# Head of a hybrid decoder block: a third weight chunk is loaded before x, first loads are cut in two, half of the token parts are made in quarters

## The chip, the core and the metric

The kernel runs on one core of a Trainium2 chip. The core has a matrix engine (TensorE, PE in the profile, with its weight loads as PEld), a vector engine (VectorE, DVE), an activation engine (ScalarE, ACT), a general engine (GpSimd, POOL) and a queue that issues most of the transfers (SyncE, SP). The metric is the time of one execution on the device, in microseconds; lower is better.

## What is computed

One layer: a pre-norm with two parallel mixers (a convolution module and a sparse attention with three branches), cross-attention into 256 memory tokens, a gated feed-forward, and a last norm. There are 256 tokens of 1024 features, all in float32. Cut to what matters here, where only the start of the work is touched:

```python
h = rms_norm(x, norm_mix_g[l])
x = x + hybrid_mixer(h, w_in[l], ...)         # u = h @ w_in[:, :2048] comes first in the kernel
h = rms_norm(x, norm_x_g[l])
x = x + cross_attention(h, mem, xq_w[l], xkv_w[l], xo_w[l])

def cross_attention(h, mem, wq, wkv, wo):
    k, v = jnp.split(mem @ wkv, 2, axis=-1)   # k = mem @ wkv[:, :1024] is made first of all
    ...
```

The keys `k` of the cross-attention need only `mem` and weights, so the kernel makes them first, while `x` is being loaded and normed.

## The kernel before

**Products.** Every weight matrix is cut into chunks of 256 output columns (k0 to k3 for the keys, u0 to u7 for the convolution's input, and so on). A chunk is 1024x256 floats, 1 MiB; it is loaded in two halves of 512 KiB (lines 211-212, 219). For most chunks both operands are split into a high part (ScalarE copies with rounding, line 184, or line 303 for data) and a low part (the difference, on VectorE or GpSimd, line 186, or line 304 for data), and `rows` (line 248) issues three sweeps for each half: high by high, high by low, low by high, eight matmuls each of 128x128 weights by 256 columns (line 259). One chunk is six such sweeps, 48 matmuls. k0 alone is multiplied in plain float32 (`whole`, line 280, matmuls at line 289), straight from the loaded `mem_t` and `k0w`, so that it needs no parts.

**Start of the program.** Lines 362-364 issue eight float32 warm-up products on ones. Lines 373-374 load the memory tokens `mem_t` in four pieces of 256 KiB from ScalarE's queue. Line 375 loads k0 in four pieces of 256 KiB from SP's queue (`ahead`, line 207-210), line 376 loads k1 in two halves. Then follow on SP's queue x in two halves (line 378), two small constant tables cp of 128x186 and pp of 128x528 floats (lines 379-380), and k2, k3 and u0 (lines 381-382). The first `Sqrt` table is asked for at line 383 on ScalarE.

**Order of the work.** `kx(0)` multiplies k0 by the memory tokens. Lines 391-393 make the memory tokens' parts in two halves of four 128-row blocks each. `kx(1)` follows. Then x is squared on ScalarE (line 397), summed over its eight blocks on VectorE to two (line 399), summed over features on TensorE (the `rn` product, line 347), rooted on ScalarE (line 349) and inverted on VectorE (line 350). Eight VectorE operations scale x into `hf` (line 405), and line 407 makes the parts of the normed tokens in four pieces x0 to x3. k2, k3 and the u chunks follow.

A planner orders the instructions of each engine by the times of its own model; each engine then runs its list in that order and waits by semaphores. `first[name]` names operations behind which the split of a weight half has to stand in the list of its engine (line 183): before, the second half of k2 stands behind the root and the inverse of the norm (line 401), the second half of k3 behind x0's part and a scaling (line 409), and the first half of u0 behind the parts x2 (line 410).

Of the kernel before, what the change touches and what calls it, by code (L numbers as in the profile page):

```python
# [97 lines left out]
def tile_hybrid_block(  # L98
# [16 lines left out]
    nc = tc.nc  # L115
# [6 lines left out]
    def long(name, slot, shape=(P, NB, S), dt=F32):  # L122

        return sb.tile(list(shape), dt, tag=f"L{slot}", name=name)

    def longs(names, slots, dt=F32R):
        return [long(n, i, dt=dt) for n, i in zip(names, slots)]
# [64 lines left out]
    first, splits, paused = {}, {}, []  # L192
# [11 lines left out]
    def ahead(name, slot):  # L204

        w = held[name] = long(f"{name}w", slot, (P, NB, 256))
        if name == "k0":
            for i in range(4):
                nc.sync.dma_start(w[:, 2 * i:2 * i + 2], w0[i])
            return  # L210
        for i in range(2):
            nc.sync.dma_start(w[:, 4 * i:4 * i + 4], wst[CHUNK_AT[name]][:, 4 * i:4 * i + 4])
# [12 lines left out]
    def half(src, name):  # L225
        w = small(name, list(src.shape), tag="w", bufs=4)
        nc.sync.dma_start(w, src)
        return split(w, list(src.shape), name)
# [73 lines left out]
    def part(hi, lo, src):  # L302
        copy = nc.scalar.activation(hi, src, AF.Copy)
        low = nc.vector.tensor_tensor(out=lo, in0=src, in1=f(hi), op=ALU.subtract)
        return copy, low
# [37 lines left out]
    def rooted_all(sqs, name, tag):  # L343

        ps = aux(f"rn_{name}", [P, S], "o", 1)
        for i, sq in enumerate(sqs):
            nc.tensor.matmul(ps, lhsT=ones, rhs=sq, start=i == 0, stop=i == len(sqs) - 1)
        r = small(f"r_{name}", [P, S], tag=tag[0], bufs=tag[1])
        root = nc.scalar.activation(r, ps, AF.Sqrt, bias=eps1)
        first[name] = root, nc.vector.reciprocal(r, r)  # L350
        return r
# [18 lines left out]
    kxh, kxl = longs(("kxh", "kxl"), (4, 5))  # L370
    mem, h = (memh, meml), (hh, hl)
    mem_t, hf = longs(("mem_t", "hf"), (6, 9), F32)
    for i in range(4):
        nc.scalar.dma_start(mem_t[:, 2 * i:2 * i + 2], memt[i])
    ahead("k0", 10)
    ahead("k1", 14)
    for i in range(2):
        nc.sync.dma_start(xt_t[:, 4 * i:4 * i + 4], xt[:, 4 * i:4 * i + 4])
    nc.sync.dma_start(cpt, cp)
    nc.sync.dma_start(ppt, pp)  # L380
    for name, slot in (("k2", 12), ("k3", 11), ("u0", 13)):
        ahead(name, slot)
    roots("roots0")

    def kx(j):
        ps = gemm(f"k{j}", mem) if j else whole("k0", mem_t)
        with behind(*first["x3"] if j > 1 else ()):
            part(kxh[:, 2 * j:2 * j + 2], kxl[:, 2 * j:2 * j + 2], ps[:])

    kx(0)  # L390
    for i in range(2):
        hs = slice(4 * i, 4 * i + 4)
        part(memh[:, hs], meml[:, hs], mem_t[:, hs])
    kx(1)
    for i in range(2):
        hs = slice(4 * i, 4 * i + 4)
# [1 line left out]
    for n in (4, 2):  # L398
        nc.vector.tensor_tensor(out=sq[:, 0:n], in0=sq[:, 0:n], in1=sq[:, n:2 * n], op=ALU.add)
    r1 = rooted_all([sq[:, 0], sq[:, 1]], "1", ("sg", 3))  # L400
    first["k2_1"] = first["1"]
    for i in range(4):
        hs = slice(2 * i, 2 * i + 2)
        for kb in (2 * i, 2 * i + 1):
# [2 lines left out]
        first[f"x{i}"] = part(hh[:, hs], hl[:, hs], hf[:, hs])  # L407
        if i == 2:
            first["k3_1"] = first["x0"][0], vec
    for name, i in (("u0_0", 2), ("u0_1", 3), ("u1_0", 3), ("u1_1", 3)):  # L410
        first[name] = first[f"x{i}"]
    for j in range(2, 4):
        kx(j)
# [885 lines left out]
    for i in range(early):  # L1299
# [4 lines left out]
        else:  # L1304
            for c in range(2):
                w = half(wfo[i, :, 2 * c:2 * c + 2], f"fo{i}_{c}")
# [9 lines left out]
    for i in range(early, NF // 2):  # L1316
        w = half(wfo[i, :, 0:2], f"fo{i}_0")
# [180 lines left out]
```

## Time and profile before

| | us |
|---|---|
| median of 3 runs | 531.47 (531.02 to 531.73) |
| the profiled execution, its own time | 532.03 |
| its span, from the first to the last instruction | 530.0 |
| TensorE busy in the span | 522.3 |
| VectorE busy | 433.9 |
| ScalarE busy | 343.7 |
| GpSimd busy | 156.0 |

The profile gives for every engine its busy time in the span. Matmuls overlap and their ends are modelled, so small holes between starts don't show as idle time of TensorE; starts of successive groups show them. A row of the timeline has the start in us, the length in us, the engine, the line, the operation, the tiles (out<-in), the shapes, a count, and in brackets the idle time of the engine just before with what ended it. A line such as L184 or L259 belongs to a helper that serves many chunks, so the tile's name tells which.

### The profile page before, as it was taken

Reading aid. Unit: us, or ns where it says so; the run is one execution under the profiler, and the core shown is the slowest. Engines: PE = TensorE matmul, PEld = TensorE weight load, DVE = VectorE, ACT = ScalarE, POOL = GpSimd, SP = SyncE. Lnnn points to the kernel's source line nnn. Section 1 sums busy time; section 2 is a strip of 40 time slices with the busy share of each in tenths; the row PEclk is TensorE's granted clock in tenths of the full one; section 3 lists DMA queues with packets and bytes.
Section 4 is the critical chain, followed back from the end, with each engine's and each line's share of the span. In section 5 each row is a group of like instructions: output and inputs, shape, how many; then the busy total and the mean of one; then the engine's idle time right before and its main releaser. Section 6 shows DMA issues by size and latency. Waiting matters only on the chain.

```text
span 530.0 us, 11121 instructions
## 1 busy us (share of the span) xinstructions
PE 522.3 (99%) x4316; PEld 504.8 (95%) x4316; DVE 433.9 (82%) x871; ACT 343.7 (65%) x599; POOL 156.0 (29%) x110
## 2 busy tenths in 40 slices
PE   9999999999999999999999999999999999999995
PEld 8999999999999999999999999999999999988884
DVE  4868999899978898975869676697889888878985
ACT  4685466787656888789446664665556665657553
POOL 0069999999961200200004000330000000000001
PEclk9999999999999999999999999999999999999998
DMA  8927954664355544347765643847765567455622
GB/s 309 416 98 267 350 185 161 202 216 160 121 182 177 178 141 135 105 147 213 233 205 171 235 153 119 236 167 258 218 199 198 198 233 226 157 137 173 220 88 80
DMA packets 30740, 101.55 MB, mean 192 GB/s; under 512 B 3296, under 2 KB 5856, under 8 KB 30304
## 3 DMA queue, kind: packets, MB, share of 16 engines
q1 hardware_dynamic: 29104, 96.99, 54.0%
q0 software_dynamic: 864, 2.62, 3.1%
q10 hardware_dynamic: 720, 1.23, 0.6%
q8 instruction: 34, 0.56, 0.5%
q14 instruction: 18, 0.15, 0.1%
HBM read 99.59 MB, written 1.25 MB: 190 GB/s over the span
## 4 chain that ended last, share of the span: by engine, by line
PE 60%; DVE 1%; ACT 0%; issue 0%; ACTq 0%; DVEq 0%
PE ps_f L259 23%; PE fo L1254 6%; PE ps_xo L259 4%; PE ps_v L259 4%; PE ps_pw L259 4%; PE ps_wo L259 4%; PE ps_xq L259 4%; PE m L1254 4%; PE xs L989 1%; PE xo_ps L989 1%; PE o L819 1%; PE pt_a L798 1%; PE s L753 1%; PE o L816 1%; PE pt_b L798 0%; PE o L810 0%
## 5 line engine op out<-in xcount | busy, mean ns | idle before, releaser
L437 DVE SCALAR_TENSOR_TENSOR yp<-vt,ppt,yp 128x256 f32<-128x256 f32 x204 | 81.6, 480 | 0.2
L259 PE MATMUL ps_f<-g,f_1h 128*128 128x256 f32 x352 | 44.4, 277 | 0.0
L259 PE MATMUL ps_f<-g,f_0h 128*128 128x256 f32 x352 | 43.8, 277 | 0.0
L259 PEld LDWEIGHTS ps_f<-g,f_1h 128*128 128x128 f32 x352 | 42.1, 188 | 0.1
L259 PEld LDWEIGHTS ps_f<-g,f_0h 128*128 128x128 f32 x352 | 41.8, 188 | 0.0
L184 ACT ACTIVATE f_0h<-f 128x1024 fp32r<-128x1024 f32 x22 | 23.3, 1057 | 16.8 <-issue 5.7
L186 DVE TENSOR_TENSOR f_1l<-f,f_1h 128x1024 fp32r<-128x1024 f32 x22 | 27.4, 1248 | 6.8 <-ACT f_1h L184 5.9
L184 ACT ACTIVATE f_1h<-f 128x1024 fp32r<-128x1024 f32 x22 | 23.3, 1060 | 14.3 <-PE ps_f L259 10.6
L186 DVE TENSOR_TENSOR f_0l<-f,f_0h 128x1024 fp32r<-128x1024 f32 x22 | 26.7, 1212 | 1.7 <-ACT f_0h L184 1.7
L186 POOL TENSOR_TENSOR u_0l<-u,u_0h 128x1024 fp32r<-128x1024 f32 x7 | 17.4, 2479 | 30.4 <-DVE kt L523 30.4
L259 PE MATMUL ps_f<-g,f_0l 128*128 128x256 f32 x176 | 23.9, 277 | 0.0
L259 PE MATMUL ps_f<-g,f_1l 128*128 128x256 f32 x176 | 23.7, 277 | 0.0
L259 PEld LDWEIGHTS ps_f<-g,f_0l 128*128 128x128 f32 x176 | 21.9, 188 | 0.0
L1220 DVE TENSOR_TENSOR ab<-ps_f,r 128x512 f32<-128x512 f32 x22 | 15.1, 689 | 8.3 <-PE ps_f L259 8.3
L259 PEld LDWEIGHTS ps_f<-g,f_1l 128*128 128x128 f32 x176 | 21.7, 188 | 0.0
L773 ACT ACTIVATE p<-p,mins 128x256 f32<-128x256 f32 x32 | 15.9, 502 | 8.4 <-DVE mins L758 8.4
L1138 POOL DMA_DIRECT2D spare<-in_wfo_dram x1 | 0.9, 866 | 65.1 <-DVE ab L1220 65.1
L186 POOL TENSOR_TENSOR u_1l<-u,u_1h 128x1024 fp32r<-128x1024 f32 x7 | 17.9, 2560 | 0.0
L449 POOL TENSOR_TENSOR yt<-yt,vw 128x512 f32<-128x512 f32 x13 | 17.1, 1312 | 0.0
L1222 ACT ACTIVATE sl<-ab 128x256 f32<-128x256 f32 x22 | 9.1, 417 | 11.1 <-DVE ab L1220 11.1
L1296 POOL TENSOR_TENSOR x<-y,gf 128x512 f32<-128x512 f32 x2 | 2.6, 1298 | 46.1 <-issue 46.1
L259 PE MATMUL ps_u<-hh,u_0h 128*128 128x256 f32 x128 | 16.1, 276 | 0.0
(614 smaller groups left out, 1632.1 us busy)
## 6 DMA issues: line engine op xcount, KB each, us to landing
f<-in_wst_dram SPq DMA_DIRECT2D x44, 512.0 KB, 4.3
fo<-in_wfo_dram SPq DMA_DIRECT2D x16, 512.0 KB, 3.5
u<-in_wst_dram SPq DMA_DIRECT2D x14, 512.0 KB, 7.9
q<-in_wst_dram SPq DMA_DIRECT2D x8, 512.0 KB, 4.1
ga<-in_wst_dram SPq DMA_DIRECT2D x8, 512.0 KB, 3.5
gc<-in_wst_dram SPq DMA_DIRECT2D x8, 512.0 KB, 3.7
v<-in_wst_dram SPq DMA_DIRECT2D x8, 512.0 KB, 5.8
pw<-in_wst_dram SPq DMA_DIRECT2D x8, 512.0 KB, 4.8
```

What stands on the lines that cost most here:

```text
L184: copy = nc.scalar.activation(hi, w, AF.Copy)
L186: splits[name] = copy, eng.tensor_tensor(out=lo, in0=w, in1=f(hi[:]), op=ALU.subtract)
L259: mm = nc.tensor.matmul(ps[:, b], lhsT=lhsT, rhs=rhs, start=row + b + kb == 0, stop=kb == NB - 1 and row == 2 and b == 1)
L437: nc.vector.scalar_tensor_tensor(out=out[:, i] if t == ts[-1] else acc[i], in0=v, scalar=w, in1=acc[i], op0=ALU.mult, op1=ALU.add)
L449: nc.gpsimd.tensor_tensor(out=yt[:, 0:2], in0=yt[:, 0:2], in1=pr, op=ALU.add)
L753: nc.tensor.matmul(s1, lhsT=qh(hd, 1), rhs=t[:, g].rearrange("p b t -> p (b t)"), start=i == 0, stop=i == 1)
L773: exp.append(nc.scalar.activation(p1[k][:, br], p1[k][:, br], AF.Exp, scale=-1.0, bias=mins[:, hd, 1, br:br + 1], accum_out=sums[:, hd, 1, ...
L798: mm = nc.tensor.transpose(ps[:, i], src, ident)
L989: mm = nc.tensor.matmul(o, lhsT=lhsT, rhs=rhs, start=n == 0, stop=n == len(order) - 1)
L1220: scaled[:] = [nc.vector.tensor_tensor(out=ab, in0=ps, in1=rf.unsqueeze(1).to_broadcast([P, 2, S]), op=ALU.mult)]
L1222: silu = nc.scalar.activation(sl, ab[:, 0], AF.Silu)
L1254: mm = nc.tensor.matmul(o, lhsT=a[x], rhs=b[w], start=start and n == 0, stop=stop and n == 2)
```

## The change

It does five things, all in the first microseconds of the program: the first of k0's four pieces and the first of the memory tokens' four pieces are loaded as two single blocks each; k2 is loaded ahead of x on SP's queue; the second half of the memory tokens' parts is made in two quarters; the split of k2's second half no longer has to stand behind the norm's root and inverse; and the split of u0's first half stands behind the parts x1 instead of x2.

```diff
         if name == "k0":
-            for i in range(4):
+            for k in range(2):
+                nc.sync.dma_start(w[:, k], w0[0, :, k])
+            for i in range(1, 4):
                 nc.sync.dma_start(w[:, 2 * i:2 * i + 2], w0[i])
             return
...
-    for i in range(4):
+    for k in range(2):
+        nc.scalar.dma_start(mem_t[:, k], memt[0, :, k])
+    for i in range(1, 4):
         nc.scalar.dma_start(mem_t[:, 2 * i:2 * i + 2], memt[i])
     ahead("k0", 10)
     ahead("k1", 14)
+    ahead("k2", 12)
     for i in range(2):
         nc.sync.dma_start(xt_t[:, 4 * i:4 * i + 4], xt[:, 4 * i:4 * i + 4])
     nc.sync.dma_start(cpt, cp)
     nc.sync.dma_start(ppt, pp)
-    for name, slot in (("k2", 12), ("k3", 11), ("u0", 13)):
+    for name, slot in (("k3", 11), ("u0", 13)):
         ahead(name, slot)
...
     kx(0)
-    for i in range(2):
-        hs = slice(4 * i, 4 * i + 4)
+    for hs in (slice(0, 4), slice(4, 6), slice(6, 8)):
         part(memh[:, hs], meml[:, hs], mem_t[:, hs])
     kx(1)
...
     r1 = rooted_all([sq[:, 0], sq[:, 1]], "1", ("sg", 3))
-    first["k2_1"] = first["1"]
...
-    for name, i in (("u0_0", 2), ("u0_1", 3), ("u1_0", 3), ("u1_1", 3)):
+    for name, i in (("u0_0", 1), ("u0_1", 3), ("u1_0", 3), ("u1_1", 3)):
         first[name] = first[f"x{i}"]
```

## The prediction

> **What bounds the kernel now.** I read the page first: the span's engines, and the chain of work that ended last.
>
> ```profile
> span 530.0 us, 11121 instructions
> ...
> PE 522.3 (99%) x4316; PEld 504.8 (95%) x4316; DVE 433.9 (82%) x871; ACT 343.7 (65%) x599; POOL 156.0 (29%) x110
> ...
> PE 60%; DVE 1%; ACT 0%; issue 0%; ACTq 0%; DVEq 0%
> ```
>
> TensorE is busy for 522.3 of 530.0 us, and no other engine has a share of the chain worth the name. So the change can win only what TensorE loses before the u chunks, and it can lose whatever it makes TensorE wait. Next came the view by stretches, to see whether a hole lies in the part that the change touches. Its columns are the stretch, its length, busy time and count of each engine, the granted clock, the DMA share and its rate.
>
> ```profile
> core 0: us, PE busy (x) PEld busy (x) DVE busy (x) ACT busy (x) POOL busy (x), PEclk, DMA share, GB/s
> 5.00:10.00 5.00, 5.00 (x24) 4.21 (x24) 1.34 (x2) 2.13 (x3) 0.00 (x0) 1.00 1.02 392
> ...
> 15.00:20.00 5.00, 4.53 (x35) 4.25 (x35) 4.17 (x5) 3.27 (x5) 0.00 (x0) 1.00 1.02 415
> ```
>
> The second of these stretches has the hole (4.53 of 5.00); the clock is whole and the transfers run all the time (share 1.02). TensorE's timeline shows where it is:
>
> ```profile
> 4.37 7.20 PE L289 MATMUL ps_k<-mem_t,k0w 128*128 128x256 f32 x32
> ...
> 15.18 1.10 PE L259 MATMUL ps_k<-meml,k_1h 128*128 128x256 f32 x8
> 16.12 1.10 PE L259 MATMUL ps_k<-memh,k_1l 128*128 128x256 f32 x8
> 17.70 1.10 PE L347 MATMUL rn<-xtsq,ones 128*128 128x256 f32 x4 [0.47 <-DVE xtsq L399]
> 18.45 1.28 PE L259 MATMUL ps_k<-memh,k_0h 128*128 128x256 f32 x8
> 19.57 1.07 PE L259 MATMUL ps_k<-meml,k_0h 128*128 128x256 f32 x8
> 20.48 1.07 PE L259 MATMUL ps_k<-memh,k_0l 128*128 128x256 f32 x8
> ```
>
> A sweep of eight takes 0.94 us from start to start in k1 (15.18 to 16.12). The next could have started at 16.12 + 0.94 = 17.06, and the norm's product starts at 17.70. So 0.64 us is lost (0.47 is what the modelled ends leave of it), because x's sum of squares is late and k2's weights, which could have filled the time, come after x. That is the largest sum at stake: 0.64 of 532.03 us of the profiled execution's own time, 0.12%. The same rows show two paces: 0.94 us for eight in k1, 0.91 in k2.
>
> ScalarE's timeline tells when the transfers land, since several of its operations wait for nothing else:
>
> ```profile
> 2.63 1.28 ACT L171 ACT_TABLE_LOAD   x1 [2.63 <-issue]
> ...
> 5.58 1.06 ACT L303 ACTIVATE memh<-mem_t 128x1024 fp32r<-128x1024 f32 x1 [1.45 <-DMA mem_t<-in_memt_dram]
> 8.80 1.06 ACT L303 ACTIVATE memh<-mem_t 128x1024 fp32r<-128x1024 f32 x1 [2.16 <-DMA mem_t<-in_memt_dram]
> 9.98 1.06 ACT L184 ACTIVATE k_0h<-k1w 128x1024 fp32r<-128x1024 f32 x1
> ...
> 13.21 1.06 ACT L397 ACTIVATE xtsq<-xtsq 128x1024 f32<-128x1024 f32 x1 [0.43 <-DMA xtsq<-in_xt_dram]
> 14.51 1.06 ACT L397 ACTIVATE xtsq<-xtsq 128x1024 f32<-128x1024 f32 x1 [0.23 <-DMA xtsq<-in_xt_dram]
> 16.65 1.06 ACT L184 ACTIVATE k_0h<-k2w 128x1024 fp32r<-128x1024 f32 x1 [1.08 <-DMA k2w<-in_wst_dram]
> ...
> 20.17 1.04 ACT L184 ACTIVATE k_0h<-k3w 128x1024 fp32r<-128x1024 f32 x1
> ...
> 25.75 1.14 ACT L303 ACTIVATE hh<-hf 128x512 fp32r<-128x512 f32 x2
> 26.79 1.05 ACT L184 ACTIVATE u_0h<-u0w 128x1024 fp32r<-128x1024 f32 x1
> ```
>
> x's halves land at 13.21 and 14.51, so 512 KiB take 1.30 us; k2's first half lands at 16.65, behind cp, pp and x.
>
> **The change, part by part.** *k2 ahead of x.* k2's halves take x's places in the queue and land at 13.2 and 14.5. High part 1.06, low part about 1.2 (VectorE rows below): ready at 15.5 and about 16.8. TensorE wants the first at 17.06 and the second three sweeps later, so k2 follows k1 without a hole: **0.64 us won**. The norm's product keeps its own time (17.70 to 18.45) and moves into k2. x comes two halves later, at 15.8 and 17.1; everything behind k2 and x in SP's queue (k3, u0, u1) has the same bytes ahead of it as before, and lands as before.
>
> What the late x costs is read from VectorE, and from TensorE where it first needs the normed tokens:
>
> ```profile
> 15.60 1.95 DVE L399 TENSOR_TENSOR xtsq<-xtsq 128x1024 f32<-128x1024 f32 x2 [1.45 <-ACT xtsq L397]
> ...
> 19.49 1.74 DVE L350 RECIPROCAL r<-r 128x256 f32<-128x256 f32 x1
> ...
> 22.22 1.21 DVE L186 TENSOR_TENSOR k_0l<-k3w,k_0h 128x1024 fp32r<-128x1024 f32 x1
> 23.35 3.25 DVE L405 SCALAR_TENSOR_TENSOR hf<-xtsq,ppt,r 128x256 f32<-128x256 f32 x8
> ...
> 28.26 1.28 DVE L304 TENSOR_TENSOR hh<-hf,hh 128x512 fp32r<-128x512 f32 x2
> 29.46 1.22 DVE L186 TENSOR_TENSOR u_0l<-u0w,u_0h 128x1024 fp32r<-128x1024 f32 x1
> ```
>
> ```profile
> 28.64 1.30 PE L259 MATMUL ps_u<-hh,u_0h 128*128 128x256 f32 x10
> 29.77 1.07 PE L259 MATMUL ps_k<-memh,k_1l 128*128 128x256 f32 x8
> ...
> 31.36 1.07 PE L259 MATMUL ps_u<-hh,u_0l 128*128 128x256 f32 x8
> ```
>
> Before, the inverse ends at 21.23 and the scaling `hf` starts only at 23.35, because VectorE makes low parts of k2 and k3 in between. These 2.1 us are the cover under which x may be late: k2's low parts now go into VectorE's idle time before 15.60 and just after it. The new chain: squares end at 17.1 + 1.06 = 18.2, sums at 20.15; the norm's product starts 0.15 later as before (15.60 + 1.95 = 17.55 to 17.70), the inverse 1.79 after that (17.70 to 19.49), at 22.1, and ends at 23.85. In the gap at 20.15 to 22.1 VectorE can make k3's first low part, whose high part ends at 21.2: it then runs from 21.2 to 22.4 and puts the inverse off to 22.4 to 24.15. So `hf` starts between 23.85 and 24.15, and at 24.7 if TensorE finishes a further sweep of k2 before the norm's product. I take 24.1, the nearest to the order of before, which lets a ready low part go first: 0.75 later than before.
>
> From there: u0's high part stood 3.44 behind hf's start (26.79 - 23.35). It now passes one of the two x parts in the 1.14 us row, 0.57, and ends at 24.1 + 3.44 - 0.57 + 1.05 = 28.0. TensorE arrives at 28.64 - 0.64 = 28.0: no slack left, no wait. u0's low part stood 6.11 behind hf, passes one 0.64 low part, and ends at 24.1 + 6.11 - 0.64 + 1.22 = 30.8; TensorE arrives at 31.36 - 0.64 = 30.7. That is **0.1 us of new waiting**. The rest of TensorE's list (k3, u1 and on) only shifts.
>
> *k2 at k1's pace.* Three or four sweeps of k2 now run on without a break from k1, at 0.94 instead of 0.91 us: **0.1 us lost**. Whether the break at the norm's product then brings the faster pace is a rival below.
>
> *k0 and the memory tokens in pieces.* k0's products follow the warm-up without an idle time (the row at 4.37 has none in brackets), so an earlier landing wins nothing there. Later in k0 there is one small hole, for the third piece:
>
> ```profile
> 7.85 3.32 PEld L289 LDWEIGHTS ps_k<-mem_t,k0w 128*128 128x128 f32 x16 [0.24 <-issue]
> ```
>
> It bounds both sides: at best 0.24 us of weight-load idle goes (about 0.1 for the products), and any delay of the third piece falls on TensorE in full. Four more places in two queues move the same bytes; I take zero. On each queue the extra issue costs a share of these rows, 0.45 us:
>
> ```profile
> 0.74 1.86 ACTq L374 DMA_DIRECT2D mem_t<-in_memt_dram  x4
> 0.75 1.81 SPq L209 DMA_DIRECT2D k0w<-in_w_dram  x4
> 4.26 0.80 SPq L212 DMA_DIRECT2D k1w<-in_wst_dram  x2
> ```
>
> k1's issue, the ninth, comes only at 4.26 though the eighth ended by 2.6, so it waits for a free place. With ten small loads the fifth on ScalarE's queue may wait likewise; behind it stand the table load (then up to 4.3 to 5.6 instead of 2.63) and `memh`, at 5.58 now. Even 0.3 us there is covered: `memh` is not used before k1, which follows k0's end at 11.6 (4.37 + 7.20).
>
> [...]
>
> *The second half of the memory parts in quarters.* One 1.06 us copy becomes two of 0.57, the first already when the third piece has landed. ScalarE idles 2.16 us before 8.80, and k1's high part waits for its weights until 9.98; both hide it. Without that cover it would cost 0.1 us. Zero.
>
> Sum: -0.64 + 0.1 + 0.1 = **-0.45 us**, 532.03 to 531.6 for the profiled execution, 531.47 to **531.0** for the median. The likeliest case's own range is 530.5 (no new wait, k0's hole closed) to 531.5 (the gain eaten by u0's wait).
>
> **The rivals.** *The slower pace stays (slower).* These pieces of the chain and this stretch show what the pace is worth:
>
> ```profile
> 331.30 14.13 PE ps_xo L259 x120
> ...
> 352.22 10.60 PE ps_f L259 x90
> ...
> 370.34 97.92 PE ps_f L259 x864
> ```
>
> ```profile
> 19.23:72.95 53.72, 53.72 (x476) 53.72 (x475) 1.00 0.71 257
> ```
>
> 118 ns a matmul in the first two, 113 in the third and in the stretch after the norm's product (53.72/476), at the same clock of 1.00. So the pace is a state that a stage takes up after a break and keeps. Before, the stretch behind the norm's product got the fast one. If the product, now in the midst of k2, leaves the slow one until the stage ends at 72.95, 476 matmuls cost 4.3 ns more each: +2.05, so 533.05. For it: after the same product at 352.22 the slow pace did stay. Against: it needs to last through every wait of k3 and u0. It decides from 0.64 us up, that is if it lasts for 150 matmuls. Chance 0.10.
>
> [...]
>
> *x is too late (same to slower).* Each 0.1 us that `hf` starts after 24.0 costs 0.1. If the whole 2.60 us pass through (25.95), u0 waits 1.9 longer, and the net is +1.4: 532.9. For it: all the cover lies on one engine, VectorE, and hangs on the planner's order. Against: 2.1 of the 2.6 us are covered by count. Chance 0.10, of which 0.04 above 0.2%.
>
> *The small pieces are slow (same).* If the four pieces of 128 KiB ran at half the 392 GB/s, their 512 KiB would take 2.7 us instead of 1.3, k0's third piece would be 1.3 late, and the net is +0.85: 532.3. Chance 0.05. [...]
>
> *The change does not do what it says (slower).* If the planner leaves ScalarE's squares of x ahead of k2's split, k2's high part starts at 18.2 and k2 at 19.3, with the norm's product still to come: 0.85 + 0.86 us later than now, 533.2. Chance 0.04.
>
> *Later stages change their pace (faster).* Everything later shifts by half a microsecond, so stages may take up the other pace. The two stretches at 118 ns in the rows above hold 210 matmuls; at the fast pace they would be 0.9 us shorter, which with the likeliest sum gives -1.35, 530.1; other stages may flip too, in both directions, so I put this case at 529.6 to 530.4. Chance 0.24.
>
> **How the numbers follow.** The likeliest case has 0.47. About 0.2%, 1.06 us, can be told from no change here: the three runs lie 0.13% apart. Faster by more: 0.24. Within: 0.47 + 0.06 + 0.05 = 0.58. Slower by more: 0.10 + 0.04 + 0.04 = 0.18. The range leaves out most of the two slowest cases and the far end of the fastest: 529.9 to 532.6.
>
> **What would show it.** Right: k2's first sweep starts 0.94 us after k1's last, without a bracket; the norm's product lies inside k2; `hf` starts near 24.1; u0's first row near 28.0; no bracket over 0.2 us on TensorE up to 73 us. Wrong: u0's rows at 28.6 or later (x too late); sweeps of 0.94 us in the u chunks (pace); the row at 4.37 or the hole at 7.85 later by 0.3 or more (pieces); a first hole of TensorE behind k1 (order). A gain or loss over 1 us without any of these must lie in the later stages' pace.

## The result, and the profile after

| | before | after |
|---|---|---|
| median, us | 531.57 (530.97 to 531.96, 6 runs) | 537.17 (535.68 to 537.85, 6 runs) |
| ratio | | 1.0099, interval 1.0079 to 1.0118 |
| profiled execution, its own time | 532.03 | 535.68 |
| its span | 530.0 | 533.9 |
| TensorE busy | 522.3 | 522.1 |

The change makes the kernel slower by 1.0%, 5.6 us; forecast were 531.0 and a range that ends at 532.6. The profiled execution is the fastest of the six, 3.65 us above the profiled one before. TensorE is busy in it as long as before (522.1 us, in a longer span), so what was lost in it is waiting. TensorE's timeline of the changed kernel shows where:

```profile
4.63 2.31 PE L291 MATMUL ps_k<-mem_t,k0w 128*128 128x256 f32 x8
7.97 5.42 PE L291 MATMUL ps_k<-mem_t,k0w 128*128 128x256 f32 x24 [1.04 <-DMA mem_t<-in_memt_dram]
13.04 1.29 PE L261 MATMUL ps_k<-memh,k_0h 128*128 128x256 f32 x8
...
17.94 1.11 PE L261 MATMUL ps_k<-memh,k_1l 128*128 128x256 f32 x8
18.89 1.10 PE L261 MATMUL ps_k<-memh,k_0h 128*128 128x256 f32 x8
...
23.59 1.11 PE L261 MATMUL ps_k<-memh,k_1l 128*128 128x256 f32 x8
24.54 1.02 PE L349 MATMUL rn<-xtsq,ones 128*128 128x256 f32 x4
25.21 1.29 PE L261 MATMUL ps_k<-memh,k_0h 128*128 128x256 f32 x8
...
27.29 1.10 PE L261 MATMUL ps_k<-memh,k_0l 128*128 128x256 f32 x8
30.44 1.19 PE L261 MATMUL ps_k<-memh,k_1h 128*128 128x256 f32 x8 [2.05 <-ACT k_1h L184]
...
32.38 1.30 PE L261 MATMUL ps_u<-hh,u_0h 128*128 128x256 f32 x10
...
39.33 1.20 PE L261 MATMUL ps_u<-hh,u_1l 128*128 128x256 f32 x8 [0.79 <-DVE u_1l L186]
```

k2 does follow k1 without a hole (17.94 to 18.89, one sweep), as the change says. But the norm's product, at 17.70 before, is at 24.54: all six sweeps of k2 stand ahead of it. Behind it come only three sweeps of k3 (25.21 to 27.29), then two holes with brackets, 2.05 and 0.79, and u0 starts at 32.38 instead of 28.64. Was x's sum not there earlier? VectorE's and ScalarE's timelines of the changed kernel:

```profile
20.66 1.95 DVE L403 TENSOR_TENSOR xtsq<-xtsq 128x1024 f32<-128x1024 f32 x2 [0.26 <-ACT xtsq L401]
...
26.11 1.75 DVE L352 RECIPROCAL r<-r 128x256 f32<-128x256 f32 x1 [2.36 <-ACT r L351]
27.90 3.26 DVE L408 SCALAR_TENSOR_TENSOR hf<-xtsq,ppt,r 128x256 f32<-128x256 f32 x8
```

```profile
16.47 1.06 ACT L401 ACTIVATE xtsq<-xtsq 128x1024 f32<-128x1024 f32 x1 [0.18 <-DMA xtsq<-in_xt_dram]
19.09 0.60 ACT L305 ACTIVATE kxh<-ps_k 128x512 fp32r<-128x512 f32 x1 [1.55 <-PE ps_k L261]
19.58 1.05 ACT L401 ACTIVATE xtsq<-xtsq 128x1024 f32<-128x1024 f32 x1
...
25.60 0.47 ACT L351 ACTIVATE r<-rn,eps_t 128x256 f32<-128x256 f32 x1 [4.03 <-PE rn L349]
28.81 0.63 ACT L305 ACTIVATE hh<-hf 128x512 fp32r<-128x512 f32 x1 [2.73 <-DVE hf L408]
29.35 1.04 ACT L184 ACTIVATE k_1h<-k3w 128x1024 fp32r<-128x1024 f32 x1
```

The sums end at 20.66 + 1.95 = 22.61, and the product comes 1.93 us later: it does not wait for x, it waits its turn in TensorE's list. From it a chain runs over root, inverse, `hf` and x0's part to the split of k3's second half (29.35 + 1.04 = 30.39), which its mark holds behind x0: 30.44 - 24.54 = 5.90 us, and meanwhile TensorE has the product itself and three sweeps of k3 to do, 3.7 us. ScalarE's and VectorE's idle time meanwhile (4.03 and 2.36 us) shows that nothing else kept them. A second point is on ScalarE: the second square of x, at 19.58, stands behind `kxh`, the high part of k1's result (19.09), which waits 1.55 us for k1's last product.

### The profile page after: what moved, and what is told of

Same layout as the page of the kernel before. It is cut to its first block, busy times and chain, and to the rows that moved or that the text cites. A ratio compares the mean times of both kernels' runs of the same rounds, so it can differ in the third digit from the quotient of the medians.

```text
span 533.9 us, 11131 instructions
## 1 busy us (share of the span) xinstructions
PE 522.1 (98%) x4316; PEld 504.1 (94%) x4316; DVE 433.4 (81%) x872; ACT 344.2 (64%) x600; POOL 156.3 (29%) x110
## 4 chain that ended last, share of the span: by engine, by line
PE 60%; DVE 1%; ACT 0%; issue 0%; ACTq 0%; DVEq 0%
PE ps_f L261 22%; PE fo L1257 6%; PE ps_v L261 4%; PE ps_pw L261 4%; PE ps_xo L261 4%; PE ps_wo L261 4%; PE ps_xq L261 4%; PE m L1257 4%; PE xs L992 1%; PE xo_ps L992 1%; PE o L822 1%; PE pt_a L801 1%; PE s L756 1%; PE o L819 1%; PE pt_b L801 0%; PE o L813 0%
## 5 line engine op out<-in xcount | busy, mean ns | idle before, releaser
L186 POOL TENSOR_TENSOR u_1l<-u,u_1h 128x1024 fp32r<-128x1024 f32 x7 | 17.8, 2544 | 0.0
```

Source lines behind the costliest of these rows:

```text
L186: splits[name] = copy, eng.tensor_tensor(out=lo, in0=w, in1=f(hi[:]), op=ALU.subtract)
```

## The experiments

Theory A: the loss comes from the place of the norm's product behind all of k2, from where its chain is no longer covered. Rivals: that x itself lands too late, that the small pieces of the first loads cost it, that the pace of the products or the clock does. A letter in an expectation holds within that run's own text. All ratios are to the kernel before on the same chip.

| run | median, us | ratio, interval |
|---|---|---|
| pieces alone | 532.52 | 1.0005 (0.9983 to 1.0027) |
| without pieces | 536.10 | 1.0060 (1.0032 to 1.0089) |
| k2's mark back | 538.34 | 1.0105 (1.0074 to 1.0135) |
| half of k2 ahead | 532.71 | 1.0005 (0.9981 to 1.0028) |
| k3's mark gone | 535.08 | 1.0051 (1.0027 to 1.0075) |
| product early | 535.38 | 1.0058 (1.0032 to 1.0083) |
| product early, no pieces | 532.09 | 1.0007 (0.9982 to 1.0033) |
| quarters alone | 532.66 | 1.0004 (0.9984 to 1.0024) |
| changed kernel, second | 537.97 | 1.0109 (1.0091 to 1.0127) |
| pieces, four loads each | 534.04 | 1.0043 (1.0028 to 1.0059) |
| tokens' pieces alone | 532.49 | 1.0015 (1.0006 to 1.0023) |
| changed kernel, filled with 16 | 538.13 | 1.0118 (1.0091 to 1.0145) |
| product early, squares first | 532.37 | 1.0010 (0.9994 to 1.0027) |
| changed kernel, third | 536.88 | 1.0098 (1.0070 to 1.0125) |
| changed kernel, filled with 8 | 535.05 | 1.0064 (1.0043 to 1.0085) |
| squares first only | 537.49 | 1.0112 (1.0081 to 1.0142) |
| changed kernel, fourth | 536.35 | 1.0087 (1.0061 to 1.0112) |

### Which part costs it

**Pieces alone**: the kernel before with the first quarters of k0 and of the tokens in two pieces each (the tokens' lines are changed likewise).

```diff
-            for i in range(4):
+            for k in range(2):
+                nc.sync.dma_start(w[:, k], w0[0, :, k])
+            for i in range(1, 4):
                 nc.sync.dma_start(w[:, 2 * i:2 * i + 2], w0[i])
```

> Of the change only the cutting of the first loads is made: the first pieces of k0 and of the memory tokens come as two single blocks each, k2 stays behind x. Theory A (the loss has two sources: the pieces make a hole in k0 of about 1.0 us and start k1 about 1.8 us later; and the norm's product, put behind all six sweeps of k2, makes x's parts late, which opens the holes at 28 and 38 us): k0 has its hole again, k1 starts near 13.0 us instead of 11.2, the hole ahead of the norm's product (0.64 us) is swallowed, and the time is 1.0 to 1.3 us above before. Rival B (the pieces slow the transfers, and all the later holes follow from that): 3.5 to 5.5 us above before. Rival C (the loss is in the pace that later stages take up): k1 may start late, but the total is within 1 us of before.

532.52, no difference that can be measured, though its trace has a hole of 1.42 us in k0. The pieces alone, with k2 behind x, don't make the loss.

**Without pieces**: the change less these lines.

> The change without the cutting of the first loads: k2 ahead of x, the memory parts in quarters, both marks as changed. Theory A: k0 has no hole and k1 starts near 11.2 us; the norm's product still stands behind all of k2 and starts near 23 us; hf starts near 26, TensorE has a hole of 2 to 2.5 us ahead of the second half of k3 and one of about 0.8 in u; the time is 2.5 to 3 us above before. Rival B (pieces alone are the cause): no hole over 0.3 us behind k1, time 0.4 us below before. Rival C: no holes, but a time that moves by 1 to 2 us with the pace.

536.10, ratio 1.0060: over half of the loss stays, and the rest goes with the pieces. TensorE's timeline of that run:

```profile
22.31 1.07 PE L259 MATMUL ps_k<-memh,k_1l 128*128 128x256 f32 x8
23.22 0.39 PE L259 MATMUL ps_k<-memh,k_0h 128*128 128x256 f32 x2
23.45 1.02 PE L347 MATMUL rn<-xtsq,ones 128*128 128x256 f32 x4
...
29.35 1.50 PE L259 MATMUL ps_k<-memh,k_1h 128*128 128x256 f32 x8 [2.37 <-ACT k_1h L184]
30.65 1.91 PE L259 MATMUL ps_k<-meml,k_1h 128*128 128x256 f32 x8
32.35 1.86 PE L259 MATMUL ps_u<-hh,u_0h 128*128 128x256 f32 x10
```

The product again has all of k2 ahead of it (and two products of k3), and the same hole follows, 2.37 us. What is odd is the row after it: eight products take 1.70 us from start to start (30.65 to 32.35) instead of 0.91. That is taken up below.

On ScalarE the order is another one here. Both squares of x stand ahead of `kxh`:

```profile
16.77 1.06 ACT L397 ACTIVATE xtsq<-xtsq 128x1024 f32<-128x1024 f32 x1 [0.17 <-DMA xtsq<-in_xt_dram]
17.98 0.60 ACT L303 ACTIVATE kxh<-ps_k 128x512 fp32r<-128x512 f32 x1
```

With the pieces alone they do so too (squares from 14.61, `kxh` at 19.28). So the planner turns this order round only where the pieces and k2 ahead of x come together, and then the second square ends at 20.6 instead of 17.8.

**k2's mark back**: the whole change, with k2's second half behind the norm's root and inverse again.

```diff
     r1 = rooted_all([sq[:, 0], sq[:, 1]], "1", ("sg", 3))
+    first["k2_1"] = first["1"]
```

> The change with one line put back: the split of k2's second half stands again behind the root and the inverse of the norm. TensorE's list then has the norm's product behind three sweeps of k2 instead of six. Theory A: k0's hole is there (k1 near 13.0 us); TensorE waits about 1 us for the norm's product near 22.7, hf starts near 26.3 instead of 27.9; u0's first sweep, which now stands ahead of three sweeps of k3, waits about 2 us; in all 4 to 4.5 us above before, a little less than the change. If the place of the norm's product is all that matters behind k0: 1.5 us above before. Rival B: as the change, 4 to 5.6 above.

538.34, ratio 1.0105, more than the 4 to 4.5 us that A expected here. The product moves forward to 22.89, and the loss is no smaller: now k2's second half waits for its own split, which the mark holds behind that product.

```profile
22.89 1.10 PE L349 MATMUL rn<-xtsq,ones 128*128 128x256 f32 x4 [0.89 <-DVE xtsq L403]
25.50 1.19 PE L261 MATMUL ps_k<-memh,k_1h 128*128 128x256 f32 x8 [1.51 <-ACT k_1h L184]
...
31.28 1.19 PE L261 MATMUL ps_u<-hh,u_0h 128*128 128x256 f32 x8 [0.97 <-ACT u_0h L184]
```

So the dropped mark by itself is not the fault; k2 ahead of x needs it dropped, and needs the product early as well.

**Half of k2 ahead**: the kernel before with k2's first half loaded ahead of x and its second half where it was, and both marks as changed.

```diff
     ahead("k1", 14)
+    ahead("k2", 12, (0,))
...
-    for name, slot in (("k2", 12), ("k3", 11), ("u0", 13)):
+    ahead("k2", 12, (1,))
+    for name, slot in (("k3", 11), ("u0", 13)):
```

> A version between: no cut pieces and no quarters; only the first half of k2 is loaded ahead of x (512 KiB, so x is 1.3 us later instead of 2.6), the second half behind the small tables; both marks as in the change. Theory A: the hole ahead of the norm's product is filled by three sweeps of k2, the product stands behind them near 20 us, hf starts near 24.1, holes of 0.5 us at most ahead of k3's second half; time between 0.5 below and 0.3 above before. Rival B: 0.4 below before, no hole. If any delay of x costs in full: about 1 us above before.

532.71, ratio 1.0005. The product is at 21.20 between k2's halves, and TensorE's timeline has no bracket behind it. Nothing is lost, and nothing is won.

**Quarters alone**: the kernel before with the later half of the tokens' parts in quarters and u0's first half behind x1.

> The kernel before with only the later half of the tokens' parts in quarters and u0's first half marked behind x1 instead of x2. Both theories: these parts lie beside TensorE's work in the kernel before, so within 0.4 us of it. Rival D (the small instructions cost): one more instruction on ScalarE and on VectorE ahead of k1's second half and of x's squares, 0.3 to 0.5 us each, which shift k1's second half or the product: 0.5 to 1 above the kernel before.

532.66, ratio 1.0004 (0.9984 to 1.0024): no cost of these two parts can be told.

### Is it the place of the product?

**k3's mark gone**: the changed kernel without the mark that holds k3's second half.

```diff
-        if i == 2:
-            first["k3_1"] = first["x0"][0], vec
```

> The changed kernel without the mark that holds the split of k3's second half behind x0. Theory A (late chain): in the changed kernel the norm's product stands on TensorE behind all six sweeps of k2 (24.54 us), and the chain from it over r, the inverse, hf, hh and the split of k3's second half takes until 30.4, while only three sweeps of k3 are left to cover it; the mark hands this delay to k3. ScalarE and VectorE stand idle between 22 and 25 us, so without the mark the split is done there, the 2.05 us before k3's second half go, and u0's first sweep, which needs hh, waits at most 0.5 in their place: 1.8 to 2.8 us below the changed kernel, 2.4 to 3.8 above the kernel before. Rival B (late x): whatever is unmarked, u0 must wait for hf, which is late by x's own landing; the hole only moves: within 0.7 of the changed kernel, 4.9 or more above the kernel before.

535.08, 2.1 below the changed kernel's first median (2.6 by the ratios), as A expects. In TensorE's timeline k3 now runs through, and the holes behind it are small:

```profile
28.40 1.07 PE L261 MATMUL ps_k<-memh,k_1h 128*128 128x256 f32 x8
...
31.50 2.14 PE L261 MATMUL ps_u<-hh,u_0h 128*128 128x256 f32 x16 [0.23 <-ACT u_0h L184]
33.81 1.21 PE L261 MATMUL ps_u<-hh,u_0l 128*128 128x256 f32 x8 [0.17 <-DVE u_0l L186]
```

**Product early**: the whole change, with k2's second half and k3's first put behind the norm's product (`first["rn1"]`) in TensorE's list.

```diff
-            sweep(ps, halved(name, i), x, i, nat, name in in_order)
+            w = halved(name, i)
+            with behind(*first["rn1"] if (name, i) in (("k2", 1), ("k3", 0)) else ()):
+                sweep(ps, w, x, i, nat, name in in_order)
```

> The whole changed kernel, but TensorE's order has the norm's product between the two halves of k2 (k2's second half and k3 are put behind it). Theory A: the product waits for the sums of x until about 22.6 us (a hole of 0.8 to 1.1 behind k2's first half), then six sweeps (5.6 us) cover the chain of 5.9: the hole before k3's second half under 0.5, the one at u0's last part gone, u0's first sweep at 30.6 to 31.3 instead of 32.38: 1.5 to 2.5 us below the changed kernel, 2.8 to 4 above the kernel before. Rival B (late x): what the product gains, TensorE loses while it waits for x: within 0.7 of the changed kernel.

535.38, ratio 1.0058. In TensorE's timeline the hole before k3's second half is gone, and one of 0.89 us stands before the product:

```profile
22.89 1.10 PE L351 MATMUL rn<-xtsq,ones 128*128 128x256 f32 x4 [0.89 <-DVE xtsq L405]
...
28.38 1.07 PE L261 MATMUL ps_k<-memh,k_0l 128*128 128x256 f32 x8
29.29 1.07 PE L261 MATMUL ps_k<-memh,k_1h 128*128 128x256 f32 x8
...
31.10 1.30 PE L261 MATMUL ps_u<-hh,u_0h 128*128 128x256 f32 x10
```

**Product early, no pieces**: the same without the pieces.

> As the run with the product early, without the pieces of k0 and of the tokens, so that k1 is done about a microsecond earlier and x's squares with it. Theory A: the sums are there at 20.3 us, when k2's first half ends (20.5): no hole at the product; six sweeps cover the chain but for at most 0.5; u0's first sweep at 28.9 to 29.5: between 0.5 below and 0.9 above the kernel before, 3.4 to 4.5 us below the run that has the same parts with the product late (536.1 then). Rival B (late x): 1.5 or more above the kernel before.

532.09, ratio 1.0007. This shows one cause: against the run without pieces only the place of the product in TensorE's list differs, and the ratio falls from 1.0060 to 1.0007, 2.8 us (less than the 3.4 to 4.5 expected; 4.0 by the medians, which come from two chips). x comes behind k2 in both, so its late landing is not what costs it. TensorE's timeline has no bracket between k0 and u0:

```profile
19.86 1.07 PE L259 MATMUL ps_k<-memh,k_0l 128*128 128x256 f32 x8
20.76 1.02 PE L349 MATMUL rn<-xtsq,ones 128*128 128x256 f32 x4
21.44 1.27 PE L259 MATMUL ps_k<-memh,k_1h 128*128 128x256 f32 x8
...
28.89 1.30 PE L259 MATMUL ps_u<-hh,u_0h 128*128 128x256 f32 x10
```

Four ratios together show a second cause, the pieces:

| | with pieces | without pieces |
|---|---|---|
| product behind all of k2 | 1.0099 | 1.0060 |
| product early | 1.0058 | 1.0007 |

The place of the product is worth 2.2 us with the pieces and 2.8 without. The pieces are worth 2.1 us with the product late and 2.7 with it early, about as much, although with k2 behind x they make 1.0005. From the last trace to that of the product early with pieces, u0 starts 2.21 us later (28.89 to 31.10): k1 starts 0.79 later (12.39 to 13.18), and the product waits for x's sums, whose second square stands behind `kxh`.

**Product early, squares first**: the whole change, product early, and k1's high part (`kxh`) behind x's second square on ScalarE; the lines of the squares also stand ahead of `kx(1)` in the program.

```diff
-        with behind(*first["x3"] if j > 1 else ()):
+        with behind(*first["x3"] if j > 1 else first["sq"] if j else ()):
```

> The run with the whole change and the product early, with k1's high part put behind x's second square on ScalarE (the planner had put it ahead, so that the square waited for k1's last product). If the order on ScalarE is what the pieces' delay of k1 turns into a late product: the square ends near 18.8 instead of 20.6, the sums near 20.9 instead of 22.6, the hole of 0.89 at the product goes, u0 starts 0.7 to 1.0 earlier (30.1 to 30.4 where k1 starts at 13.18): 0.6 to 1.2 us below that run (535.38), 2.3 to 3.2 above the kernel before. If x's landing or VectorE sets it: within 0.3 of that run.

532.37, ratio 1.0010: the whole change, with two lists put right, costs nothing that can be measured. The gain over the run before it (1.0058) is 2.6 us, more than the 0.6 to 1.2 expected. The hole of 0.89 is gone. But in this run's trace k0's hole is 0.20 where it was 1.29 there, and of the 2.18 us by which u0 is earlier, 1.07 come from k1's start (13.18 to 12.11), which lies ahead of the squares. Whether that is luck of the one trace stays open, and with it how much of the 2.6 us the order on ScalarE is worth.

**Squares first only**: the same without the product early.

> The changed kernel with only the order on ScalarE mended (k1's high part behind x's second square); the norm's product stays behind all six sweeps of k2 on TensorE. Theory A (place of the product): the sums are there 1 to 1.7 us earlier and wait for TensorE; the holes behind stay at 1.8 to 2.3 us: within 0.7 us of the changed kernel, 4.5 or more above the kernel before. Rival J (order on ScalarE): the loss comes from the squares alone: 2 us or more below the changed kernel.

537.49, ratio 1.0112: no gain, as A expects. In its TensorE timeline the product is still behind all of k2, and the hole before k3's second half is 2.82 us:

```profile
24.83 1.03 PE L349 MATMUL rn<-xtsq,ones 128*128 128x256 f32 x4
...
30.73 1.20 PE L261 MATMUL ps_k<-memh,k_1h 128*128 128x256 f32 x8 [2.82 <-ACT k_1h L184]
```

ScalarE's order is worth something only once the product stands early.

### The hole that the change was to close

**Before, again** (the kernel before, profiled once more).

> The kernel before, profiled once more. In its first profile the granted clock rose at 4.085 us, ahead of k0, and k1 started at 11.22; in every later profile of a kernel without pieces it rose at 5.5 to 6.8 and k1 started at 12.1 to 12.5. If the early rise was that run's luck (theory E), k1 starts here at 12.0 to 12.6 with four to six matmuls of k0 at 427 ns, and the hole of 0.64 ahead of the norm's product is 0.2 or gone: what step 1 of the prediction meant to gain was then never there in most executions. If it belongs to the kernel, k1 starts near 11.2 and the hole is 0.5 to 0.7.

532.37, and the hole is not there. TensorE's timeline:

```profile
4.63 8.38 PE L289 MATMUL ps_k<-mem_t,k0w 128*128 128x256 f32 x32
12.66 1.27 PE L259 MATMUL ps_k<-memh,k_0h 128*128 128x256 f32 x8
...
17.40 1.07 PE L259 MATMUL ps_k<-memh,k_1l 128*128 128x256 f32 x8
18.31 1.02 PE L347 MATMUL rn<-xtsq,ones 128*128 128x256 f32 x4
18.98 1.27 PE L259 MATMUL ps_k<-memh,k_0h 128*128 128x256 f32 x8
```

k0 takes 8.38 us here and took 7.20 in the first profile. The trace's record of the granted clock starts, with 1.0, at 7.28 us here and at 4.09 there. The first six of k0's 32 matmul rows here lie ahead of it and take 427 ns each, the later ones 216, as if at half the clock. k1 ends later, and x's sums are in time for it: 17.40 + 0.91 = 18.31. The four further traces with k2 behind x (pieces alone, quarters alone, four loads each, tokens' pieces alone) have no hole there either. So the 0.64 us were seen in one execution of six, the one with the early clock. (In the four earlier profiles without pieces that the expectation speaks of, the clock rose at 6.2 to 7.0 us, not 5.5 to 6.8.)

### The pieces

**Pieces, four loads each**: pieces as above, and the last two quarters of each as one load.

```diff
-            for i in range(1, 4):
-                nc.sync.dma_start(w[:, 2 * i:2 * i + 2], w0[i])
+            nc.sync.dma_start(w[:, 2:4], w0[1])
+            nc.sync.dma_start(w[:, 4:8].rearrange("p (i k) s -> p i k s", i=2), w0[2:4].rearrange("i p k s -> p i k s"))
```

> The kernel before with the first quarter of k0 and of the tokens in two pieces, but the last two quarters of each in one load, so that each has four loads as before (with the pieces alone and five loads each, TensorE waited 1.42 us in k0 for the tokens and k1 started at 13.43). Theory F (places): the fifth load of each waits for one of eight places, and behind it the rest; with four loads each the hole in k0 is 0.5 or less, or one at the last half in its place, and k1 starts at 12.0 to 12.8. Rival G (small pieces): the pieces themselves move slowly; the hole stays at 1.0 to 1.9 and k1 at 13.0 to 13.6. The time is within 0.6 us of the kernel before in both.

**Tokens' pieces alone**: only the tokens' first quarter in two pieces.

> The kernel before with only the tokens' first quarter in two pieces (nine loads where ten were, eight places). Theory F (places): only one load waits for a place, and less of it: a hole of 0.3 to 0.9 in k0. Rival G (small pieces): half of the small pieces, half of the hole at k0, or the whole where the tokens are what TensorE waits for: 0.7 to 1.6. The time within 0.6 us of the kernel before.

Both expectations missed in part: with four loads the time is 2.3 us above the kernel before by the ratio, and with the tokens' pieces alone 0.8, where both said within 0.6. TensorE's timeline with four loads each:

```profile
8.27 1.97 PE L291 MATMUL ps_k<-mem_t,k0w 128*128 128x256 f32 x8 [0.87 <-DMA mem_t<-in_memt_dram]
10.86 3.69 PE L291 MATMUL ps_k<-mem_t,k0w 128*128 128x256 f32 x16 [0.62 <-DMA mem_t<-in_memt_dram]
```

The holes stay, and the time is 534.04, ratio 1.0043; so the wait for a free place is not the cause, or not alone (in the changed kernel's first trace the fifth loads of the tokens and of k0 are issued at 3.38 and 3.54 us, 0.8 and 1.0 after the fourths' issue ended). With the tokens' pieces alone there is no hole, and 532.49, ratio 1.0015. The transfer view of the first 12 us, of the kernel before (second profile), the pieces alone and the four loads, in this order:

```profile
DMA packets 1586, 3.71 MB, mean 309 GB/s; under 512 B 169, under 2 KB 169, under 8 KB 1586
```

```profile
DMA packets 1803, 3.45 MB, mean 288 GB/s; under 512 B 192, under 2 KB 704, under 8 KB 1803
```

```profile
DMA packets 1750, 3.38 MB, mean 282 GB/s; under 512 B 157, under 2 KB 669, under 8 KB 1750
```

About 500 packets under 2 KB more, and 0.26 to 0.33 MB less moved in the same time (0.15 to 0.22 less than in the first profile of before, which moved 3.60 MB). The two load queues took about the same share of the engines' time (85.2, 84.7 and 82.6%).

The single packets of these traces say more. The last packet of k0 and the tokens, 2 MiB together, ends at 7.8 to 8.4 us in the six traces without pieces, at 9.7 with the tokens' pieces alone, and at 9.1 to 10.7 in the thirteen traces with both kinds of pieces. So the pieces make the first loads later every time. The length of a piece's packet is not the reason: in every trace the median packet of 1 KiB takes 46 ns and that of 2 KiB 84. By these medians the 512 packets of 1 KiB in place of 256 of 2 KiB add about 0.13 us on 16 engines (an estimate). The engines' time for the same 2 MiB grows by more, from 5.7 to 6.0 us without pieces to 6.2 to 6.9 with both kinds, in packets far longer than the median. What holds those up stays open.

### The clock behind the hole

**Changed kernel, second, third and fourth**:

> The changed kernel once more. Theory A: product behind all of k2, a hole of 1.8 to 2.5 us before k3's second half and one of 0.5 to 1 in u; 536 to 538.5, 4 to 6 above the kernel before. If the holes were that one run's, they differ here by more than 0.7.

> The changed kernel beside the two others on the same chip: 536 to 538.5. Theory H: in a trace whose windows of 3.41 us, counted from the first rise of the clock, hold 1.9 us or more of the hole within one of them, the clock falls at that window's end; where the hole is split between two windows it doesn't. Rival I: no such relation.

> The changed kernel beside the two others on the same chip, as a measure for them: 536 to 538.5 by every theory.

537.97, 536.88 and 536.35. The holes are there each time (2.14 us before k3's second half in all three), and the slow products behind them come and go. The view by stretches of the third and then of the fourth, in stretches of 3.41 us (the time that the fall in the third lasts) from the clock's first rise (7.13 and 5.32 us); the column behind POOL's is the granted clock:

```profile
27.60:31.02 3.42, 1.28 (x11) 1.08 (x10) 3.38 (x10) 2.39 (x4) 0.00 (x0) 1.00 0.04 18
31.02:34.43 3.41, 3.41 (x18) 3.41 (x18) 3.41 (x5) 3.41 (x6) 0.00 (x0) 0.50 0.00 0
```

```profile
25.80:29.21 3.41, 2.27 (x21) 2.07 (x19) 3.29 (x5) 0.67 (x3) 0.00 (x0) 1.00 0.45 184
29.21:32.62 3.41, 2.41 (x21) 2.41 (x22) 3.41 (x8) 3.41 (x7) 0.00 (x0) 1.00 0.00 0
```

In the third, the whole hole lies in one stretch (TensorE busy 1.28 of 3.42), and through the next the clock is at 0.50, with 18 products instead of 31 in the stretch after it. In the fourth the hole is split between two stretches (2.27 and 2.41 busy), and the clock stays. All six traces with such a hole agree (the changed kernel's four, without pieces, squares first only): it fell with 2.05, 2.14 and 2.37 us of idle time in one stretch and not with 1.82 or less. The three falls come 23.893, 23.893 and 27.307 us after the first rise, seven, seven and eight times 3.413, and each lasts 3.413 us. That the idle time of each such stretch decides the clock of the next is a reading of these six traces, none of which has an idle time between 1.82 and 2.05 us in a stretch.

**Changed kernel, filled**: sixteen, then eight products of 128 columns in the hole.

```diff
+            if name == "k3" and i:
+                fill = aux("fill", [P, P], "o", 1)
+                for _ in range(16):
+                    with in_line():
+                        mm = nc.tensor.matmul(fill, lhsT=ones, rhs=ones, start=True, stop=True)
+                last[:] = [mm]
```

> The changed kernel with sixteen further products of 128 columns (107 ns each at full clock, 1.7 us together) on TensorE between k3's first half and its second, whose result nobody reads: they fill the hole of 2.05 to 2.14 us and delay nothing. Theory H (clock): in two of three traces with that hole (the changed kernel's second, the one without pieces) the granted clock fell to 0.5 for 3.41 us about a microsecond after it, worth 1.7 us; in the changed kernel's first trace it did not, and its runs lie in two groups, 535.7 and 537.0 to 537.9. Filled, the clock does not fall in any run: median 1.0 to 2.0 us below the changed kernel's, no run above 536.8, and the granted clock stays at 1.0 from k0 on. Rival I (later pace): the two groups come from the paces of later stages; the median stays within 0.5 of the changed kernel's and the runs spread as before.

> The changed kernel with eight further products in the hole before k3's second half; sixteen of them took 3.49 us (218 ns each, not the 107 that had been reckoned) and pushed k3's second half back by 1.2 to 1.4, so eight take 1.75 and stay inside the 2.1. Theory H (clock): the granted clock doesn't fall behind the hole in any run; the median is 0.5 to 1.5 us below that of the changed kernel beside it, and its upper group goes. Rival I (pace): with the hole filled the run with sixteen still came to 538.1 less 1.3 = 536.8, the changed kernel's own 536.9; then the median here is within 0.4 of the changed kernel's.

Sixteen took 3.49 us, 32 matmul rows of 109 ns, instead of 1.7: a product takes two rows, and the 107 ns of the expectation, an estimate, is near the time of one. The run (538.13) tells nothing of the theory but that the clock then didn't fall (a mean of 0.999 in its trace). Eight: 535.05, 1.3 below the changed kernel on the same chip, as H expects, but the intervals of the two ratios overlap (1.0043 to 1.0085, 1.0061 to 1.0112). The mean granted clock is 0.995 or less in 14 of the changed kernel's 22 runs, in none of the 8 filled ones and in none of the kernel before's beside them, which speaks for a fall in most runs of the changed kernel. What it is worth isn't separated: half of 3.41 is 1.7 us where it happens (an estimate), the 14 runs have a median of 537.4 and the other eight of 536.6, and in the trace of the filled run the hole of 0.8 in u has gone too.

## Why the prediction was wrong

- **The step that failed: "hf starts between 23.85 and 24.15, and at 24.7 if TensorE finishes a further sweep of k2 before the norm's product".** It took the product to run when its sums are there, with one sweep of delay at most. But the planner's list of TensorE had the product behind all six sweeps of k2, and the engine keeps to its list: product at 24.54, 1.93 us after its sums, `hf` at 27.90. Moving the product alone took the ratio from 1.0060 to 1.0007 without pieces, and from 1.0099 to 1.0058 with them.
- **"TensorE, where it first needs the normed tokens"** was put at u0. It is k3's second half, which a mark (line 409 before) holds behind x0; the first hole, 2.05 us, is there. Removing the mark won 2.1 us by the medians.
- **x later, covered by VectorE's 2.1 us.** The late x was indeed harmless: with the product early and no pieces the kernel is at 1.0007 with k2 still ahead of x. The second square came later than reckoned (19.58, not 17.1) since `kxh` stands ahead of it, with k1 itself 1.8 us later than in the profile of before. Without pieces, where it stands ahead of `kxh`, it started at 16.77.
- **-0.64 for the hole behind k1.** Closed, as predicted, but it was seen only in the first profile: the second one of before has none. This fits that even the versions put right are no faster than before.
- **Pieces at zero: the second step that failed.** "Four more places in two queues move the same bytes; I take zero." They do move the same bytes, but the last of them later in every trace (9.1 to 10.7 us instead of 7.8 to 8.4). Alone the pieces measure 1.0005, where u0 starts 0.8 later than in the second profile of before, which is inside that interval. With k2 ahead of x they cost 2.1 us with the product late (the intervals overlap a little, but the changed kernel's four ratios are all 1.0087 or more against 1.0060) and 2.7 with it early. Two paths are seen: k1 starts later, and the planner puts x's second square behind `kxh`. How the cost divides between them isn't settled.
- **Quarters and u0's mark at zero.** Right within the interval: 1.0004 (0.9984 to 1.0024).
- **The rivals.** "x is too late" had the right victim, `hf`, but bounded its delay by x's own 2.60 us; the list made it 4.55. "The slower pace stays" is seen in single traces (half of k2 ahead: 0.94 us a sweep to the end of u), and not in the changed kernel's first one, whose u runs at 113 ns. Its 4.3 ns a matmul is a little low: the rows beside it give 4.4 to 4.9. "The small pieces are slow" came near in mechanism, with late first loads, at half the rate for the pieces, which the packets don't show. The one rival on the planner's order looked at ScalarE's list, not at TensorE's. A fall of the granted clock wasn't among the rivals.

From the second profile of before to the first of after, u0 is 3.22 us later: 0.38 from k1's start (12.66 to 13.04), about 0.4 from twelve sweeps at 0.94 instead of 0.91, and 2.24 at the first hole (27.29 to 30.44, less one sweep of 0.91); 0.2 are left over. The second hole takes 0.9 more, 4.1 together. Where the clock falls, up to 1.7 (the estimate above) come on top, so the 5.6 of the medians lies between, but the sum isn't closed: the two profiled executions lie only 3.3 us apart.

## What to carry to other kernels

Before a load is moved ahead of the start of a dependency chain, find where the chain's first product then stands in its engine's list, and count the work left behind it against the chain's length: here 5.9 us of chain had nine sweeps behind it before, and three after. Marks that were harmless (k3's behind x0) become the place where a late chain stops the engine, so follow every one of them. Measure parts of a change together as well as alone: the pieces cost nothing that could be told by themselves and over 2 us beside the earlier k2. And a hole seen in one profile is worth a second profile before it is made the gain: this one came with an early rise of the clock (4.09 us, against 7.28 in the second).

## What was not expected of the hardware

- The granted clock's record first shows 1.0 at 4.1 to 7.3 us in the 20 traces of nearly the same program; until then a matmul row of 256 columns in k0 takes 427 ns instead of 216.
- It fell back to half for 3.41 us in the three traces where 2.05 us or more of one 3.41 us stretch were idle, and not in the three with 1.82 or less.
- A packet of 1 KiB takes 46 ns in the median and one of 2 KiB 84, yet four loads of 128 KiB in place of two of 256 KiB end the first 2 MiB 0.7 to 2.9 us later.
- A plain float32 product of 128x128 by 128 columns takes two matmul rows of 109 ns each, 218 ns (3.49 us for sixteen).
